# Expert weights in wide row chunks: one group of four chunks for two units of a mixture-of-experts stage

## The chip, the cores and the metric

The kernel runs on one core of a Trainium2 chip. The metric is the device time of one execution in microseconds (us). Before the change the median of three runs is 1634.07 us (1633.24 to 1634.15).

## The reference

Two transformer layers over 512 tokens of width 1024, in float32. Layer 0 is sliding-window attention with a dense SwiGLU; layer 1 is a forgetting attention with a mixture of experts: each token goes to the best 2 of 8 experts. Per expert e and its tokens xb:

```
h = xb @ w_in[e]                      # 1024 -> 2 x 2816 (gate half, up half)
y = (silu(h[:, :2816]) * h[:, 2816:]) @ w_out[e]     # 2816 -> 1024
```

The outputs are weighted with the gates, added per token, and a layer norm closes the layer. The float32 products have to be kept close to float32 accuracy.

## The kernel before, in words

Each float32 matrix is split into a high and a low float16 part, and a product is three matmuls (high·high, high·low, low·high). The weights stream from HBM for this. Class `Weights` (lines 81 to 178) keeps a list of *chunks* of at most 2096 columns per partition. `load` (SP's queue) brings a chunk into a raw buffer (3 buffers, and 4 more in the expert stage); `upper` makes the high part on ScalarE (ACT, line 149), in pieces of 1048 columns; `lower` makes the low part on VectorE (DVE, line 158), one piece behind (`LAG`). The high and low parts live in `NHL` = 7 buffers; a chunk may take a buffer only when the chunk seven places before it has been freed (`W.free`, which sets `done`). `need(i)` demands chunk i before its matmuls.

The conversions have no schedule of their own. The program order is written out by hand: TensorE's (PE's) matmuls are emitted, and between them `tick()` (line 1651) emits one pending small job, one step of `chores`, and one or two conversion pieces: two if fewer than `LEAD` chunks are converted beyond `done`, else one. Each engine then works through its own list in order.

The expert stage (lines 1733 to 1798) runs over 8 expert slots with a fixed number of token columns, `CAP` = 160, 128, 152, 134, 144, 140, 168, 128. A slot's first product is cut in 11 *units*. Units 0 to 9 alternate gate and up, 512 weight columns each: `block4` holds 2 chunks of 4 row blocks x 512 columns, 96 matmuls, 4 ticks. Unit 10 (`gate_pair`) does the last 256 columns of both halves together. After a gate unit ACT applies SiLU to the PSUM result (line 1457); after an up unit DVE multiplies (line 1458), ACT makes the high part and GpSimd (POOL) the low part (line 1460); `pend` holds these and each of the following ticks emits one. The PSUM tile of a unit is reused two units later. Then `down_wide` does the second product, with chunks of 2 row blocks x 1024 columns; the last slot uses `down_direct`.

`chores` (line 1624) is the leftover of the routing: its second step computes the gates (DVE, with one exponential on ACT), its third splits them into three float16 parts (lines 1610 to 1618), the next four scale rows on ACT. `places`, `fetch`, `own_gates` and `ready` prepare the tokens of the next slot after units 2, 4, 6 and 8; `jobs` adds the normalisation of finished rows in the last two slots. When the stage begins, the first three chunks have been loaded and converted by earlier ticks.

Of the kernel before, what the change touches and what calls it, by code (L numbers as in the profile page):

```python
# [8 lines left out]
FT = mybir.dt.float32  # L9
# [11 lines left out]
KD = D // 128  # L21
FF = 2816
# [35 lines left out]
CMAX = max(CAP)  # L58
# [14 lines left out]
BO = "m0mm1m23"  # L73
NHL = 7
LAG = 1
LEAD = 4
QUADS = KF // 4
KG = ((0, 8), (8, 7), (15, 7))


class Weights:
# [87 lines left out]
    def need(self, i):  # L169
        while self.hcut <= i:  # L170
            self.tick(1, force=True)
        while self.cut <= i:
            self.lower()
        return self.chunks[i][3]

    def free(self, u, n=None):

# [32 lines left out]
def trunk_kernel(ctx, tc, x, mem, positions, w_in_swa, attn_sinks, w_in_fox, b_forget, w_mem_kv, w_out,  # L210
                 ln_attn_g, ln_attn_b, w_ffn_in, w_ffn_out, w_router, b_router, w_exp_in, w_exp_out,
                 ln_ffn_g, ln_ffn_b, out):
    nc = tc.nc
# [13 lines left out]
    def bank2():  # L227
        return ps.tile([128, 2, 512], FT, name="bk2", tag="S", bufs=2)

    def high(o, i, scale=1.0):  # L230
        nc.scalar.activation(o, i, AF.Copy, scale=scale)  # L231
# [13 lines left out]
    W = Weights(nc, rawp, hlp)  # L245
# [18 lines left out]
    def unit(u, n):  # L264
        return [View(W, u, i, n) for i in range(2)]
# [33 lines left out]
    u_ei, u_eo = [], []  # L299
    W.from_ = len(W.chunks)  # L300
    def add_exp(s, which, *parts):
        return W.add(*((lambda s=s, k=k, c=c: exp_of(s, which)[:, k[0]:k[1], c[0]:c[1]],
                        (k[1] - k[0]) * (c[1] - c[0])) for k, c in parts))

    for s in range(NEXP):
        u_ei.append([add_exp(s, 0, *[((k, k + 4), (c, c + 512)) for k in (0, 4)])
                     for q in range(QUADS) for c in (512 * q, FF + 512 * q)])
        u_ei[s].append(add_exp(s, 0, *[((0, KD), (c + 512 * QUADS, c + 512 * QUADS + 256)) for c in (0, FF)]))
        if s < LAST:
            u_eo.append([add_exp(s, 1, *[((k, k + 2), (0, D)) for k in range(k0, min(k0 + 4, KF), 2)])  # L310
                         for k0 in range(0, KF, 4)])
        else:
            u_eo.append([add_exp(s, 1, ((k0, k1), (c, c + 512)), ((k1, k0 + kn), (c, c + 512)))
                         for c in (0, 512) for k0, kn in KG for k1 in (k0 + (kn + 1) // 2,)])
# [636 lines left out]
    for i, u in enumerate(u_fi):  # L951
# [16 lines left out]
        else:  # L968
            for jj in range(2):
                f = slice(jj * 128, jj * 128 + 128)  # L970
                b = bank2()
# [417 lines left out]
    def gate_pair(pool, C, w, xe, act, i, tick, nj=2):  # L1389

        wh, wl = w
        b = bank2()
        for jj in range(nj):
            f = slice(jj * 128, jj * 128 + 128)
            for s in range(2):
                for k in range(KD):
                    mm3(b[:, jj, s * C:s * C + C], wh[:, s, k, f], wl[:, s, k, f], xe[0][:, k, :C], xe[1][:, k, :C],
                        k == 0, k == KD - 1)
                tick()

        b = b[:, :nj]
        sa = pool.tile([128, 4, CMAX], FT, name="sa", bufs=nj)[:, :nj]
        j = slice(nj * i, nj * i + nj)

        def first():
            nc.scalar.activation(sa[:, :, :C], b[:, :, :C], AF.Silu, scale=DS)

        def second():
            nc.vector.scalar_tensor_tensor(sa[:, :, :C], b[:, :, C:2 * C], DS * SA, sa[:, :, :C], op0=OP.mult,
                                           op1=OP.mult)  # L1410

        def third():
            high(act[0][:, j, :C], sa[:, :, :C])

        def fourth():
            low(act[1][:, j, :C], sa[:, :, :C], 1.0, act[0][:, j, :C])
        return first, second, third, fourth
# [12 lines left out]
                nc.tensor.matmul(o, wl[:, k, f], act[0][:, kk, :C], start=False, stop=lastk, skip_group_check=True)  # L1430
            tick()

    def block4(C, u, xe, b, tick):

        wh, wl = unit(u, 512)
        for kk in (0, 4):
            for f in range(4):
                o = b[:, f // 2, (f % 2) * C:(f % 2) * C + C]
                c = slice(f * 128, f * 128 + 128)
                for k in range(kk, kk + 4):  # L1440
                    first = k == 0 and f % 2 == 0
                    nc.tensor.matmul(o, wh[:, k, c], xe[0][:, k, :C], start=first, stop=False, skip_group_check=True)  # L1442
                    nc.tensor.matmul(o, wh[:, k, c], xe[1][:, k, :C], start=False, stop=False, skip_group_check=True)  # L1443
                    nc.tensor.matmul(o, wl[:, k, c], xe[0][:, k, :C], start=False, stop=k == KD - 1,  # L1444
                                     skip_group_check=True)
                if f % 2:
                    tick()
            if kk == 0:
                W.free(u, 1)

    def quad(C, b, up, sa, act, q):

        v = b[:, :, :2 * C].rearrange("p a (f c) -> p a f c", c=C)
        sv = sa[:, :, :C].rearrange("p (a f) c -> p a f c", f=2)
        j = slice(4 * q, 4 * q + 4)
        if not up:
            return [lambda: nc.scalar.activation(sv, v, AF.Silu, scale=DS)]
        return [lambda: nc.vector.scalar_tensor_tensor(sv, v, DS * SA, sv, op0=OP.mult, op1=OP.mult),  # L1458
                lambda: high(act[0][:, j, :C], sa[:, :, :C]),
                lambda: nc.gpsimd.tensor_sub(act[1][:, j, :C], sa[:, :, :C], act[0][:, j, :C])]  # L1460

    def down_wide(C, u, act, acc, k0, kn, tick):
        wh, wl = unit(u, D)
# [187 lines left out]
    def tick():  # L1651
        if pend:
            pend.pop(0)()
        next(chores, None)
        W.tick(1 if W.hcut >= W.done + LEAD else 2)

# [76 lines left out]
    for s in range(NEXP):  # L1733
        C = CAP[s]
        act = [mx.tile([128, KF, CMAX], FH, name=f"act{i}", bufs=1) for i in range(2)]
        for i, u in enumerate(u_ei[s]):
            if i < 2 * QUADS:
                if i % 2 == 0:
                    sa = mx.tile([128, 4, CMAX], FT, name="sa", bufs=2)
                b = bank2()  # L1740
                block4(C, u, XE[s], b, tick)
                rest = quad(C, b, i % 2, sa, act, i // 2)
            else:
                rest = gate_pair(mx, C, unit(u, 256), XE[s], act, 2 * QUADS, tick)
            W.free(u)
            pend.extend(rest)
            if (s, i) == (0, 2):
                for _ in range(2):
                    next(chores, None)
                G[0] = own_gates(0, oh, bank())  # L1750
            if (s, i) == (0, 0):
                oh = places(me, lambda t: posm[:, t, 0:1], CAP[0])
            if (s, i) == (0, 1):
                _, _, *at_[0] = fetch(me, oh, blocks(0), False)
            if s + 1 < NEXP:
                if i == 2:
                    oh = places(me, lambda t: posS[:, t, s + 1:s + 2], CAP[s + 1])
                if i == 4:
                    rows, _, *at_[s + 1] = fetch(me, oh, blocks(s + 1))
                if i == 6:  # L1760
                    G[s + 1] = own_gates(s + 1, oh, bank())
                if i == 8:
                    ready(s + 1, rows)
            for f in jobs.get((s, i), ()):
                f()
        if s < LAST:
            acc = [bank() for _ in range(4)]
            for gi, u in enumerate(u_eo[s]):
                kn = min(4, KF - 4 * gi)
                down_wide(C, u, act, acc, 4 * gi, kn, tick)  # L1770
                W.free(u)
                for f in jobs.get((s, 11 + gi), ()):
                    f()
            pend.extend(rows_out(s, C, acc, G[s], at_[s][1]))
        else:
            for gi, u in enumerate(u_eo[s]):
                h, (k0, kn) = gi // 3, KG[gi % 3]
                if k0 == 0:
                    acc = [bank() for _ in range(1 + h)]
                last = k0 + kn == KF  # L1780

                def rest(c0, c1, acc=acc, h=h):
                    for q in range(c0, c1, 256):
                        c, i = slice(512 * h + q, 512 * h + q + 256), 2 * h + q // 256
                        v = acc[1][:, :256] if h and q else acc[0][:, q:q + 256]
                        pend.append(lambda c=c, i=i, v=v: (join(X[s][0], C, c, v, g7[:C, :], st7[:C, 6 * i:6 * i + 6]),
                                                           nc.scalar.activation(yl[:C, c], v[:C], AF.Identity, scale=g7[:C])))
                    if h:
                        late_work()

                down_direct(C, unit(u, 512), act, acc, k0, kn, tick, ((0, 256), (256, 512)) if h else ((0, 512),),
                            rest if last else None)
                W.free(u)
                for f in jobs.get((s, 11 + gi), ()):
                    f()
# [121 lines left out]
```

## Time and profile before

| | |
|---|---|
| median of three runs | 1634.07 us |
| the profiled execution | 1634.23 us, span 1632.4 us |
| mean granted TensorE clock | 0.993 |
| busy: PE, PE weight load, DVE, ACT, POOL | 1578.6, 1267.8, 1210.9, 950.3, 267.7 us |
| HBM read | 355.08 MB |

Times in the profile are microseconds from the span's start. The expert stage takes from 789 us to the end. A busy matmul engine is not one at its peak, since matmuls overlap; the distance from one start to the next says more. A wait is the idle time just before an instruction, with the one whose end released it.

### The profile page before, as it was taken

What the parts mean: (1) busy time and instruction counts of PE and PEld (TensorE: products, weight loads), DVE (VectorE), ACT (ScalarE), POOL (GpSimd) and SP (SyncE); (2) the same over time, 40 slices, a digit from 0 to 9 for tenths busy, and PEclk for the clock granted to TensorE, in tenths of its full rate; (3) what the DMA queues carried; (4) which work ended last, traced back from release to release, by engine and by line L of the source; (5) the groups of instructions that cost most, each with busy time, mean ns of one, the idle gap of its engine ahead of it and who ended that gap; (6) DMA issues with size and microseconds to landing.
All of it is one profiled execution on the core that took longest, in us unless ns stands there. A gap on an engine that the chain in (4) does not pass through costs nothing. (4 is left out here: it accounts for less than half of the span.)

```text
span 1632.4 us, 42978 instructions
## 1 busy us (share of the span) xinstructions
PE 1578.6 (97%) x18640; PEld 1267.8 (78%) x18640; DVE 1210.9 (74%) x1811; ACT 950.3 (58%) x1447; POOL 267.7 (16%) x264
## 2 busy tenths in 40 slices
PE   7998999999999999999899999999999999999996
PEld 6775654444444747765899999999999999999984
DVE  6798543333634568787898798888979889699997
ACT  6676243333211356663676787767877678666773
POOL 0443100000200000003120330203112030130251
PEclk9999999999999999999999999999999999999998
DMA  7511043332631132201899899999999999999993
GB/s 275 178 53 53 27 129 104 103 104 91 219 114 60 53 129 92 66 27 65 308 363 364 293 394 377 352 370 305 390 357 361 375 320 373 329 297 360 358 369 113
DMA packets 180549, 370.16 MB, mean 227 GB/s; under 512 B 6589, under 2 KB 49597, under 8 KB 180352
## 3 DMA queue, kind: packets, MB, share of 16 engines
q1 hardware_dynamic: 173280, 343.48, 58.6%
q0 software_dynamic: 4768, 15.47, 4.0%
q10 hardware_dynamic: 2304, 8.39, 1.4%
q8 instruction: 148, 2.42, 0.6%
q14 instruction: 49, 0.40, 0.1%
HBM read 355.08 MB, written 12.39 MB: 225 GB/s over the span
## 5 line engine op out<-in xcount | busy, mean ns | idle before, releaser
L158 DVE SCALAR_TENSOR_TENSOR wl<-raw,wh 128x1048 f16<-128x1048 f32 (+3 forms) x658 | 794.7, 1258 | 100.3 <-ACT wh L149 100.1
L149 ACT ACTIVATE wh<-raw 128x1048 f16<-128x1048 f32 (+3 forms) x658 | 641.8, 1036 | 101.7 <-PE bk L239 42.9
L1444 PE MATMUL bk<-xa,wl 128*128 128x160 f16 (+3 forms) x1280 | 260.0, 231 | 0.9 <-DVE wl L158 0.9
L1442 PE MATMUL bk<-xa,wh 128*128 128x160 f16 (+3 forms) x1280 | 260.1, 231 | 0.8 <-ACT xa L231 0.8
L1443 PE MATMUL bk<-xa,wh 128*128 128x160 f16 (+3 forms) x1280 | 260.0, 231 | 0.0
L1443 PEld LDWEIGHTS <-wh 128*128 128x128 f16 x2560 | 250.5, 98 | 3.6 <-issue 2.4
L1444 PEld LDWEIGHTS <-wl 128*128 128x128 f16 x2560 | 250.5, 98 | 1.3 <-DVE wl L158 1.1
L1442 PEld LDWEIGHTS <-wh 128*128 128x128 f16 x2560 | 250.4, 98 | 0.7
L1473 PE MATMUL bk<-act,wl 128*128 128x160 f16 (+6 forms) x1232 | 235.3, 227 | 1.2 <-DVE wl L158 1.2
L1472 PE MATMUL bk<-act,wh 128*128 128x160 f16 (+6 forms) x1232 | 235.3, 227 | 0.0
L1471 PE MATMUL bk<-act,wh 128*128 128x160 f16 (+6 forms) x1232 | 235.2, 227 | 0.0
L1442 PE MATMUL bk<-xe,wh 128*128 128x128 f16 (+2 forms) x1280 | 223.2, 221 | 2.2 <-DVE sa L1458 1.4
L1443 PE MATMUL bk<-xe,wh 128*128 128x128 f16 (+2 forms) x1280 | 223.1, 221 | 0.0
L1444 PE MATMUL bk<-xe,wl 128*128 128x128 f16 (+2 forms) x1280 | 223.1, 221 | 0.0
L237 PE MATMUL bk<-xTh,wh 128*128 128x512 f16 (+2 forms) x656 | 204.8, 322 | 1.2 <-DVE Kx L234 0.9
L239 PE MATMUL bk<-xTh,wl 128*128 128x512 f16 (+2 forms) x656 | 204.6, 322 | 1.4 <-DVE wl L158 1.4
L238 PE MATMUL bk<-xTl,wh 128*128 128x512 f16 (+2 forms) x656 | 204.6, 322 | 0.5 <-DVE xTl L234 0.5
L1460 POOL TENSOR_TENSOR act<-sa,act 128x512 f16<-128x512 f32 (+6 forms) x40 | 106.3, 2659 | 284.7 <-ACT act L231 284.6
L239 PEld LDWEIGHTS <-wl 128*128 128x128 f16 x944 | 92.4, 98 | 49.0 <-DVE wl L158 2.9
L237 PEld LDWEIGHTS <-wh 128*128 128x128 f16 x944 | 92.4, 98 | 48.7 <-ACT wh L149 2.0
L238 PEld LDWEIGHTS <-wh 128*128 128x128 f16 x944 | 92.5, 98 | 46.6 <-issue 1.5
L1473 PEld LDWEIGHTS <-wl 128*128 128x128 f16 x1232 | 120.5, 98 | 1.6 <-DVE wl L158 1.6
(349 smaller groups left out, 2669.2 us busy)
## 6 DMA issues: line engine op xcount, KB each, us to landing
raw<-in_w_exp_in_dram SPq DMA_DIRECT2D x176, 1024.0 KB
raw<-in_w_exp_out_dram SPq DMA_DIRECT2D x85, 1024.0 KB
raw<-in_w_ffn_in_dram SPq DMA_DIRECT2D x22, 1024.0 KB
raw<-in_w_out_dram SPq DMA_DIRECT2D x8, 1024.0 KB
raw<-in_w_ffn_out_dram SPq DMA_DIRECT2D x8, 1024.0 KB
raw<-in_w_in_fox_dram SPq DMA_DIRECT2D x8, 1024.0 KB
raw<-in_w_in_swa_dram SPq DMA_DIRECT2D x4, 896.0 KB
raw<-in_w_mem_kv_dram SPq DMA_DIRECT2D x3, 1024.0 KB
```

The lines of the kernel that those rows point to most:

```text
L149: self.nc.scalar.activation(h[:, p:e], t[:, p:e], AF.Copy, scale=SW)
L158: self.nc.vector.scalar_tensor_tensor(l, src, SW, h, op0=OP.mult, op1=OP.subtract)
L237: nc.tensor.matmul(o, lh, rh, start=first, stop=False, **kw)
L238: nc.tensor.matmul(o, lh, rl, start=False, stop=False, **kw)
L239: nc.tensor.matmul(o, ll, rh, start=False, stop=last, **kw)
L1442: nc.tensor.matmul(o, wh[:, k, c], xe[0][:, k, :C], start=first, stop=False, skip_group_check=True)
L1443: nc.tensor.matmul(o, wh[:, k, c], xe[1][:, k, :C], start=False, stop=False, skip_group_check=True)
L1444: nc.tensor.matmul(o, wl[:, k, c], xe[0][:, k, :C], start=False, stop=k == KD - 1, skip_group_check=True)
L1460: lambda: nc.gpsimd.tensor_sub(act[1][:, j, :C], sa[:, :, :C], act[0][:, j, :C])]
L1471: nc.tensor.matmul(o, wh[:, k, c], act[0][:, kk, :C], start=first, stop=False, skip_group_check=True)
L1472: nc.tensor.matmul(o, wh[:, k, c], act[1][:, kk, :C], start=False, stop=False, skip_group_check=True)
L1473: nc.tensor.matmul(o, wl[:, k, c], act[0][:, kk, :C], start=False, stop=kk == KF - 1, skip_group_check=True)
```

## The change

The first product of a slot is no longer cut in 11 units of 2 chunks. Its columns fall into three groups (1024, 1024, 768 wide), each with a gate half and an up half. One half of a group is one unit of four chunks, each 2 row blocks x the group's width. It serves two blocks: the first 512 columns, and then the rest (512, or 256 in the last group). The chunks are freed one by one during the second block. A slot so has 12 blocks in the order gate, gate, up, up for each group; the last two columns of row blocks, 256 columns, are a block of their own in the gate and in the up half, and go through `quad`, so that POOL and no longer DVE makes their low part. `LEAD` rises from 4 to 6. A block of 256 columns has 2 ticks in place of 4. `need_high` and `passes` are added, but no call uses them with other than the default.

```diff
-LEAD = 4
+LEAD = 6
+GROUPS = ((0, 1024), (1024, 1024), (2048, 768))
...
-        u_ei.append([add_exp(s, 0, *[((k, k + 4), (c, c + 512)) for k in (0, 4)])
-                     for q in range(QUADS) for c in (512 * q, FF + 512 * q)])
-        u_ei[s].append(add_exp(s, 0, *[((0, KD), (c + 512 * QUADS, c + 512 * QUADS + 256)) for c in (0, FF)]))
+        u_ei.append([add_exp(s, 0, *[((k, k + 2), (c, c + n)) for k in range(0, KD, 2)])
+                     for c0, n in GROUPS for c in (c0, FF + c0)])
...
+    def blocks_of(C, u, n, c0, nb, xe, b, tick, passes=(0, 1, 2)):
+        for kk in range(0, KD, 2):
+            a = W.first[u] + kk // 2
+            wh = W.need_high(a) if 2 not in passes else W.need(a)[0]
+            wl = None if 2 not in passes else W.need(a)[1]
+            for f in range(nb):
+                o = b[:, f // 2, (f % 2) * C:(f % 2) * C + C]
+                for k in (kk, kk + 1):
+                    c = (k - kk) * n + c0 + f * 128
+                    for p in passes:
+                        w = (wl if p == 2 else wh)[:, c:c + 128]
+                        nc.tensor.matmul(o, w, xe[p == 1][:, k, :C], start=p == 0 and k == 0 and f % 2 == 0,
+                                         stop=p == 2 and k == KD - 1, skip_group_check=True)
+            if nb == 4 or kk % 4:
+                tick()
+            if c0 + nb * 128 == n and 2 in passes:
+                W.free(u, kk // 2 + 1)
...
-                block4(C, u, XE[s], b, tick)
-                rest = quad(C, b, i % 2, sa, act, i // 2)
-            else:
-                rest = gate_pair(mx, C, unit(u, 256), XE[s], act, 2 * QUADS, tick)
-            W.free(u)
-            pend.extend(rest)
+        halves_of = [(u_ei[s][2 * g + up], n, c, min(4, (n - c) // 128), up, (c0 + c) // 128)
+                     for g, (c0, n) in enumerate(GROUPS) for up in range(2) for c in range(0, n, 512)]
+        sas = {}
+        for i, (u, n, c, nb, up, j0) in enumerate(halves_of):
+            if not up:
+                sas[j0] = mx.tile([128, 4, CMAX], FT, name="sa", bufs=2)
+            b = bank2()
+            blocks_of(C, u, n, c, nb, XE[s], b, tick)
+            pend.extend(quad(C, b, up, sas[j0], act, j0, nb))
...
-            for f in jobs.get((s, i), ()):
+            for f in jobs.get((s, i), ()) if i < 11 else ():
```

## Rows read from the trace of the kernel before

**Rows 1.** Windows, one: busy us (instructions) of PE, PEld, DVE, ACT, POOL; clock, DMA, GB/s
```profile
1100.00:1200.00 100.00, 100.00 (x1690) 99.56 (x1688) 86.32 (x90) 77.20 (x95) 20.56 (x9) 1.00 0.99 355
```
**Rows 2.** PE's waits, 786 to 1430 us, the longest: total, times, longest
```profile
PE bk L1444 <- DVE wl L158: 0.9, 1, 0.9
```
**Rows 3.** PE's waits, 1430 us to the end, all of them
```profile
PE bk L1518 <- DVE wl L158: 4.4, 3, 3.9
PE bk L1442 <- DVE sa L1458: 1.4, 1, 1.4
PE bk L1473 <- DVE wl L158: 1.2, 2, 0.9
PE bk L1442 <- ACT sa L1457: 0.8, 1, 0.8
```
**Rows 4.** Timeline of PE, first two units of the stage: start, duration, [idle before]
```profile
789.18 0.23 PE L1443 MATMUL bk<-xa,wh 128*128 128x160 f16 x1
...
799.56 0.23 PE L1443 MATMUL bk<-xa,wh 128*128 128x160 f16 x1
800.66 0.24 PE L1444 MATMUL bk<-xa,wl 128*128 128x160 f16 x1 [0.87 <-DVE wl L158]
...
804.30 1.00 PE L1351 MATMUL bk<-tid,oh 128*128 128x2 f16 x8 [0.70 <-DVE oh L1339]
805.23 0.24 PE L1442 MATMUL bk<-xa,wh 128*128 128x160 f16 x1
```
**Rows 5.** Waits of SP's DMA queue, 820 us to the end, the longest
```profile
SPq L122 <- DVE wl L158: 586.5, 233, 8.6
```
**Rows 6.** Timeline of DVE, first two units of the stage
```profile
796.11 1.25 DVE L158 SCALAR_TENSOR_TENSOR wl<-raw,wh 128x1048 f16<-128x1048 f32 x1
797.28 0.42 DVE L1162 TENSOR_TENSOR g<-ose,gateE 128x256 f32<-128x256 f32 x1
...
799.41 2.35 DVE L158 SCALAR_TENSOR_TENSOR wl<-raw,wh 128x1000 f16<-128x1000 f32 x2
```
**Rows 7.** Timeline of ACT, first two units of the stage
```profile
795.02 2.96 ACT L149 ACTIVATE wh<-raw 128x1048 f16<-128x1048 f32 x3
```
**Rows 8.** Windows (columns as in rows 1) around PE's two longest gaps
```profile
777.40:779.80 2.40, 0.00 (x0) 0.00 (x0) 2.29 (x8) 0.00 (x0) 0.00 (x0) 1.00 0.93 320
780.30:783.50 3.20, 3.20 (x36) 2.86 (x35) 1.55 (x3) 1.77 (x4) 2.31 (x2) 0.50 1.05 396
...
1606.30:1609.60 3.30, 3.11 (x16) 1.98 (x15) 3.27 (x5) 0.18 (x1) 3.30 (x1) 0.50 0.00 0
```
**Rows 9.** DVE's groups by shape, from 740 us: count, busy us, mean ns, idle before
```profile
L158 DVE SCALAR_TENSOR_TENSOR wl<-raw,wh 128x1048 f16<-128x1048 f32 x262 | 354.8, 1354 | 67.0 <-ACT wh L149 66.9
...
L158 DVE SCALAR_TENSOR_TENSOR wl<-raw,wh 128x488 f16<-128x488 f32 x4 | 2.6, 658 | 0.0
```
**Rows 10.** Timeline of DVE in slot 1 (128 columns)
```profile
917.82 5.85 DVE L158 SCALAR_TENSOR_TENSOR wl<-raw,wh 128x1000 f16<-128x1000 f32 x4
...
924.42 4.62 DVE L158 SCALAR_TENSOR_TENSOR wl<-raw,wh 128x1000 f16<-128x1000 f32 x4
928.96 0.68 DVE L1458 SCALAR_TENSOR_TENSOR sa<-bk,sa 128x512 f32<-128x512 f32 x1
```
**Rows 11.** Timeline of POOL in the same stretch
```profile
919.80 1.64 POOL L1460 TENSOR_TENSOR act<-sa,act 128x512 f16<-128x512 f32 x1
```
**Rows 12.** DVE's groups, 1446.7 to 1616.5 us, the costliest
```profile
L158 DVE SCALAR_TENSOR_TENSOR wl<-raw,wh 128x1000 f16<-128x1000 f32 (+1 forms) x103 | 124.6, 1264 | 5.0 <-ACT wh L149 5.0
```
**Rows 13.** Timelines at block 7 of slot 6: PE's last lookup before it, DVE
```profile
1453.44 0.24 PE L1668 MATMUL bk<-parts,oh 128*128 128x3 f16 x4
...
1454.60 0.15 DVE L1672 TENSOR_REDUCE gown<-bk 128x1 f32<-128x3 f32 x1
```
**Rows 14.** Windows of 5 us in slot 2 (columns as in rows 1)
```profile
1045.00:1050.00 5.00, 5.00 (x80) 5.00 (x78) 3.51 (x5) 2.91 (x4) 0.49 (x1) 1.00 1.01 406
...
1055.00:1060.00 5.00, 5.00 (x77) 4.98 (x78) 4.79 (x8) 5.00 (x9) 0.00 (x0) 1.00 0.68 243
```

More of the change, by code (lines that the diff above doesn't have):

```diff
@@ L174, in need, with need_high @@
         return self.chunks[i][3]
+    def need_high(self, i):
+        while self.hcut <= i:
+            assert self.upper(True)
+        return self.chunks[i][3][0]
     def free(self, u, n=None):
@@ L1431, in down_group, with quad @@
             tick()
[L1433 to L1437, printed above, removed]
-                o = b[:, f // 2, (f % 2) * C:(f % 2) * C + C]
[L1439 to L1455, printed above, removed]
+    def blocks_of(C, u, n, c0, nb, xe, b, tick, passes=(0, 1, 2)):
[4 more added lines that the diff above has]
+            for f in range(nb):
+                o = b[:, f // 2, (f % 2) * C:(f % 2) * C + C]
+                for k in (kk, kk + 1):
[8 more added lines that the diff above has]
+                W.free(u, kk // 2 + 1)
+    def quad(C, b, up, sa, act, j0, nb):
+        v = b[:, :nb // 2, :2 * C].rearrange("p a (f c) -> p a f c", c=C)
+        sv = sa[:, :nb, :C].rearrange("p (a f) c -> p a f c", f=2)
+        j = slice(j0, j0 + nb)
         if not up:
@@ L1458, in quad @@
         return [lambda: nc.vector.scalar_tensor_tensor(sv, v, DS * SA, sv, op0=OP.mult, op1=OP.mult),
-                lambda: high(act[0][:, j, :C], sa[:, :, :C]),
-                lambda: nc.gpsimd.tensor_sub(act[1][:, j, :C], sa[:, :, :C], act[0][:, j, :C])]
+                lambda: high(act[0][:, j, :C], sa[:, :nb, :C]),
+                lambda: nc.gpsimd.tensor_sub(act[1][:, j, :C], sa[:, :nb, :C], act[0][:, j, :C])]
     def down_wide(C, u, act, acc, k0, kn, tick):
@@ L1735, in trunk_kernel @@
         act = [mx.tile([128, KF, CMAX], FH, name=f"act{i}", bufs=1) for i in range(2)]
[L1736 to L1740, printed above, removed]
-                block4(C, u, XE[s], b, tick)
-                rest = quad(C, b, i % 2, sa, act, i // 2)
-            else:
-                rest = gate_pair(mx, C, unit(u, 256), XE[s], act, 2 * QUADS, tick)
-            W.free(u)
-            pend.extend(rest)
+        halves_of = [(u_ei[s][2 * g + up], n, c, min(4, (n - c) // 128), up, (c0 + c) // 128)
[7 more added lines that the diff above has]
+            pend.extend(quad(C, b, up, sas[j0], act, j0, nb))
             if (s, i) == (0, 2):
```

## The prediction, made before the run

> **What bounds the kernel now.** I read the busy table by windows first: in the expert stage PE is busy all the time at full clock, its weight loads too, DVE for 86 of 100 us, ACT for 77, and the DMA engines' share is 0.99 [rows 1]. Three engines and the DMA look full, so the table alone does not name the bound. The list of PE's waits does. Between 786 and 1430 us the longest wait on a conversion is 0.9 us [rows 2], and the whole last part holds 4.4 + 1.4 + 1.2 + 0.8 = 7.8 us [rows 3]. Matmuls of 160 columns start every (799.56 - 789.18) / 150 = 0.0692 us [rows 4], so they stand end to end; for 128 columns I scale to 0.0554 and for 168 to 0.0727. PE's column count is the bound, and the change leaves the number of matmuls and columns as it is. The loads are behind: SP's queue waits 586 us for a raw buffer to be given back [rows 5]. So the change can win only in the few waits, some 9 us in all, and it can lose wherever it starves PE. Three places decide: the start, the slots of 128 columns, and the end, where DVE falls behind.
>
> **The start: a loss.** Three chunks are converted when the stage begins. Before, two chunks fed a block of 96 matmuls, so three lasted one and a half blocks: chunk 3 was first wanted by block 1, and its second piece by matmul 153 (96 + 48 + 9). PE got there at 799.6 and waited to 800.66 [rows 4], since DVE's second piece of chunk 3 runs from 799.41 to about 800.6 [rows 6]. In the new form block 0 goes through all four chunks itself. Chunk 3 is wanted after 72 matmuls, at 789.18 + 71 x 0.0692 = 794.1. The tick that emits its conversion is the same one, after 24 matmuls, with the same chores ahead of it, so it comes no earlier: ACT's first piece is done at 795.02 + 2.96 / 3 = 796.0 [rows 7], DVE's at 797.4, then the third step of the chores takes DVE from 797.28 to 799.4, and the second piece ends at 800.6 [rows 6]. Of the first row block PE can do three matmuls in between, of the second two; the 78th matmul waits for 800.66. That leaves 19 of block 0 and 96 of block 1: 115 x 0.0692 = 7.96, so block 1 ends at 808.6. The token lookup then takes 805.23 - 804.30 = 0.93 [rows 4] and does not wait for DVE any more, as it did for 0.70. Block 2 starts at 809.5 and not at 805.23: **4.3 us lost**. Chunks 4 to 7 are late by nothing: their eight pieces and the four one-hot masks follow on DVE at 1.2 us a piece and end near 812, while chunk 7 is wanted at 814.
>
> There is a second cost. PE stood still for 2.4 us from 777.4, and then ran at a granted clock of 0.50 (1.2 GHz, not 2.4) for 3.2 us; after the 3.9 us gap at 1602 it ran at 0.50 for 3.3 us [rows 3, 8]. The new gap, 794.1 to 800.66 with five matmuls in it, is longer than both. If the half clock falls on the stretch after the gap, 3.4 us of it cost 1.7; if it falls into the gap, nothing. I take **1.7**, as both rows have it after the gap. The start costs 6.0 (4.3 to 6.0).
>
> **The other edits, stage in full run.** The elements converted are the same. A slot gets 8 chunks of 1536 columns (pieces of 1048 and 488) for 6 of 2048, so 4 pieces more. A piece of 488 columns takes 0.658 us and one of 1048, undisturbed, 1.25 [rows 6, 9]: (1.25 - 0.658) / 560 = 0.00106 per column, so 0.14 of the 0.658 are the piece's own, some 0.6 us per slot on DVE (1.354, the mean of all pieces of 1048, would make 0.05 of it) and nothing on PE as long as DVE keeps ahead. The low part of the last 256 columns moves from DVE (about 0.45 us, estimated from the multiplication 0.68 us at 512) to POOL. That is no plain gain: four DVE pieces take 4.62 us when alone, 5.85 when POOL's subtraction of 1.64 us lies in them [rows 10, 11], so a full subtraction holds DVE for 1.2 and one of half the size for about 0.6.
>
> In a slot of 128 columns a block takes 96 x 0.0554 = 5.3 us. The seven buffers now come free only in second halves, at 1.3, 2.7, 4.0 and 5.3 us of it. DVE begins with the first freed buffer after ACT's piece (1.3 + 0.1 + 1.1 = 2.5), does four pieces, 1.2 each, up to 7.4, and a subtraction may add 1.2; then comes the multiplication (0.7) of the block just ended, at 8.1 to 9.3. PE wants its PSUM tile back two blocks on, at 10.7. The margin is 1.4 to 2.6 us, and DVE is already behind by one or two us there: the multiplication at 928.96 starts without any wait for PE [rows 10]. I take **1.0** for all slots together; bounds are 0 (the margin holds) and 1.5 us for each of two groups in slots 1, 3, 4 and 5, 12 us.
>
> In the second product the larger `LEAD` puts 5 to 6 converted chunks ahead of PE, by a count of the ticks in the code, where it had 3 to 4. PE has two waits for low parts there, 1.2 us [rows 3]; they are in the sum of the end.
>
> **The end.** From slot 6 on DVE is the late engine: of 170 us from 1446.7 on it waits 5.0 for high parts [rows 12], and all PE's waits but one are for DVE [rows 3]. Here DVE's sum counts. When PE starts block 7 of slot 6 the new order has 19 chunks of the slot converted, the old 17 and a half: 1.5 x 2.4 = 3.6 us by a count of the ticks, and 1 us more since the old DVE is only then done with block 6's pieces (1454.6, PE's block begins at 1453.5 [rows 13]). Taken off: one more multiplication with its subtraction still to do (0.85 + 1.2), 8 pieces' overhead (1.2), two half subtractions (1.2) less the two low parts (0.9), and a new idle of 2.0, as the first buffer is freed 24 x 0.0727 = 1.7 us into the block and ACT needs 1.1, DVE having 0.85 of other work. Gains 5.5, costs 6.5. That is even within what such a sum is good for: **0**, bounds -9.5 (all 7.8 of waits and the 1.7 of half clock go) and +3.
>
> **Sum.** 1634.2 (the profiled execution, its span of 1632.4 and 1.8 around it, 0.2 above the median) + 6.0 + 1.0 + 0 = 1641.2 us.
>
> **A page on the loads.** The chunk's rows grow from 2 to 4 KB. At full demand the loads moved 406 GB/s in 5 us, and 243 where buffers were short [rows 14]. The Trainium skill, "DMA: Bandwidth & Descriptors", section "Where 436 GB/s comes from", puts HBM's limit per core at about 358 GB/s. By that rule the stage's 355 GB/s would be the bound, and rival 4 would hold; the trace does not agree, as it shows 406 over 5 us.
>
> **Rivals.**
> 1. *The deeper lead clears the end.* Against it: DVE's sum, not the order, sets that end. For it: two waits for low parts with DVE work between the pieces [rows 3]. Price: 7.8 + 1.7 back, 1641.2 - 9.5 = 1631.7, and 1630.0 if the half clock at the start is not paid. It ends faster than before once more than 7 us come back. Chance 0.15.
> 2. *The bunched conversions starve PE in the narrow slots.* 12 us in place of 1: 1652; half of it 1647. For it, DVE already late in slot 1; against it, PE has not one wait there now. Chance 0.13.
> 3. *The start does not stall*, because chunk 3 is converted sooner than I read, or the change does not act there as I think. Then 1634.2 + 1.0 - 0.9 - 0.7 = 1633.6. Chance 0.12.
> 4. *The loads set the pace*, and a gap of PE at the start is made up while they run on: 1634. The row with 243 GB/s under a busy PE speaks against it [rows 14]. Chance 0.05.
>
> The forecast has 0.55, with a range of its own from 1637.5 to 1645.
>
> **Chances.** About 0.2% (3.3 us) is what a measurement tells from no change: below 1630.8 faster, above 1637.3 slower. Faster: a third of rival 1, some of 3, and 0.04 for what I do not see, 0.12. Slower: the forecast's bulk and rival 2, 0.60. Same: the rest, 0.28. The range of 8 in 10 runs from 1632 to 1648.
>
> **What would show it.** Right: PE idle between 794 and 801 in block 0 of the first slot, waiting for `wl`; half clock behind it; block 2 near 809.5. PE's waits on the multiplication only in narrow slots, after an up block. At the end PE's waits add up to about the same. Wrong: no gap at the start; a last slot without waits for DVE; new waits of PE in every slot, above all at first blocks of a group.

## The result, and the profile after

The kernel after takes 1642.69 us (median of four runs, 1641.88 to 1643.38), beside 1633.65 for the kernel before in the same comparison (1633.15 to 1634.15). The ratio is 1.0052, 95% interval 1.004 to 1.0065: slower by 9 us. The profiled execution took 1641.88 us, its span 1639.8; mean granted clock 0.990.

To see where the time went I took, from the timelines of PE in both traces, the first matmul of each slot's first and second product, and formed the distance after minus before. A change of the distance from one mark to the next is what that stretch costs. Worked out in this way, in us, good to about 0.1:

| stretch | predicted | measured |
|---|---|---|
| ahead of the stage | 0 | -0.9 |
| slot 0, first product (the start) | +6.0 | +5.4 |
| slot 1, first product (128 columns) | +1.0 in all narrow slots | +0.7 |
| slots 2 to 5, first product of slot 6 | 0 | 0.0 |
| slot 6, second product | in the end's sum | -1.6 |
| slot 7, first product | in the end's sum | +5.9 |
| slot 7, second product, to the last instruction | in the end's sum | -2.1 |
| the end together | 0 | +2.2 |

The -0.9 lies ahead of the stage, where neither the new blocks nor `LEAD` act. Over the traces of this study the stage began between 785.6 and 788.9 us, the 788.9 being the kernel before's [rows 4]; I count from the stage's own start, which gives +8.3.

PE's waits, first from 780 to 1433 us and then from there to the end (total, times, longest), answer to [rows 2] and [rows 3]:

```profile
PE bk L1451 <- DVE wl L160: 3.6, 2, 2.7
PE bk L1451 <- ACT wh L151: 1.9, 1, 1.9
PE bk L1451 <- ACT xa L238: 0.8, 1, 0.8
PE bk L1451 <- DVE sa L1465: 0.7, 1, 0.7
...
PE bk L1499 <- ACT yt L1492: 2.9, 1, 2.9
PE bk L1525 <- DVE wl L160: 2.1, 2, 1.7
PE bk L1451 <- DVE wl L160: 1.5, 2, 0.8
PE bk L1451 <- DVE sa L1465: 0.3, 1, 0.3
```

The first two rows are the start, `xa` is the wait ahead of the stage's first matmul, the `sa` of 0.7 is slot 1, and `yt` is new: it is the lift of slot 6's output rows, in which ACT copies them out of PSUM for PE's transposes. The start in PE's timeline, beside [rows 4]:

```profile
795.23 0.31 PE L1451 MATMUL bk<-xa,wh 128*128 128x160 f16 x2 [1.88 <-ACT wh L151]
...
796.51 0.31 PE L1451 MATMUL bk<-xa,wl 128*128 128x160 f16 x1 [0.97 <-DVE wl L160]
...
799.75 0.31 PE L1451 MATMUL bk<-xa,wl 128*128 128x160 f16 x1 [2.66 <-DVE wl L160]
...
809.37 0.42 PE L1357 MATMUL bk<-tid,oh 128*128 128x2 f16 x8
809.72 0.31 PE L1451 MATMUL bk<-xa,wh 128*128 128x160 f16 x2
```

DVE's timeline, beside [rows 6], shows what it did while PE waited: the first piece of chunk 3, the chores' third step, and only then the second piece.

```profile
795.20 1.25 DVE L160 SCALAR_TENSOR_TENSOR wl<-raw,wh 128x1048 f16<-128x1048 f32 x1
796.37 0.42 DVE L1168 TENSOR_TENSOR g<-ose,gateE 128x256 f32<-128x256 f32 x1
...
798.41 0.20 DVE L1623 CAST parts<-gateS 128x32 f16<-128x32 f32 x1
798.50 5.74 DVE L160 SCALAR_TENSOR_TENSOR wl<-raw,wh 128x1000 f16<-128x1000 f32 x5
```

Windows of the start, beside [rows 8] (PE, PEld, DVE, ACT, POOL, then granted clock, DMA share, GB/s): the clock falls to 0.50 at 796.4, while PE still stands in the second of its three waits, and stays there until 803.2, some 3.4 us behind the last wait.

```profile
796.40:799.80 3.40, 0.63 (x4) 0.32 (x5) 3.16 (x11) 3.40 (x4) 0.00 (x0) 0.50 0.04 17
799.80:803.20 3.40, 3.40 (x27) 3.40 (x28) 3.40 (x4) 3.38 (x5) 0.00 (x0) 0.50 0.69 200
```

The new wait at slot 7's begin, in ACT's timeline. The store of normalised rows stands in ACT's list and waits for DVE's norm; behind it stand ten high pieces, and behind them the lift:

```profile
1524.61 0.34 ACTq L1715 DMA_DIRECT2D out_dram<-xtok  x1
1525.05 9.58 ACT L151 ACTIVATE wh<-raw 128x1048 f16<-128x1048 f32 x10 [4.10 <-PE bk L1480]
1534.54 0.76 ACT L1492 ACTIVATE yt<-bk 128x336 f32<-128x336 f32 x2
```

PE needs `yt` at 1535.02, after 2.94 us of waiting, and then has half the clock (window 1535 to 1540; in the one before it the clock fell, 0.87 in the mean):

```profile
1535.00:1540.00 5.00, 4.98 (x39) 4.81 (x40) 4.97 (x6) 3.86 (x7) 0.00 (x0) 0.50 1.03 416
```

### The profile page after: what moved, and what is told of

It reads as the page before. It is cut to its first block, busy times and chain, and to the rows that moved or that the text cites. A ratio compares the mean times of both kernels' runs of the same rounds, so it can differ in the third digit from the quotient of the medians.

```text
span 1639.8 us, 43254 instructions
## 1 busy us (share of the span) xinstructions
PE 1583.0 (97%) x18640; PEld 1271.9 (78%) x18640; DVE 1203.9 (73%) x1835; ACT 954.9 (58%) x1479; POOL 215.6 (13%) x272
## 3 DMA queue, kind: packets, MB, share of 16 engines
q8 instruction: 148, 2.42, 0.6%
## 5 line engine op out<-in xcount | busy, mean ns | idle before, releaser
L160 DVE SCALAR_TENSOR_TENSOR wl<-raw,wh 128x1048 f16<-128x1048 f32 (+4 forms) x690 | 788.8, 1199 | 119.4 <-ACT wh L151 119.0
L151 ACT ACTIVATE wh<-raw 128x1048 f16<-128x1048 f32 (+4 forms) x690 | 645.1, 995 | 128.3 <-PE bk L246 42.7
L1451 PEld LDWEIGHTS <-wh 128*128 128x128 f16 x5632 | 454.2, 98 | 5.1 <-ACT wh L151 2.1
L1451 PE MATMUL bk<-xa,wh 128*128 128x160 f16 (+3 forms) x2816 | 290.1, 232 | 2.7 <-ACT wh L151 1.9
L1451 PE MATMUL bk<-xa,wl 128*128 128x160 f16 (+3 forms) x1408 | 287.2, 232 | 3.6 <-DVE wl L160 3.6
L1451 PE MATMUL bk<-xe,wh 128*128 128x128 f16 (+2 forms) x2816 | 249.1, 222 | 1.0 <-DVE sa L1465 1.0
L1451 PE MATMUL bk<-xe,wl 128*128 128x128 f16 (+2 forms) x1408 | 246.9, 222 | 1.6 <-DVE wl L160 1.5
L1478 PEld LDWEIGHTS <-wh 128*128 128x128 f16 x1232 | 120.6, 98 | 0.0
L1479 PEld LDWEIGHTS <-wh 128*128 128x128 f16 x1232 | 120.5, 98 | 0.0
L1467 POOL TENSOR_TENSOR act<-sa,act 128x512 f16<-128x512 f32 (+13 forms) x48 | 65.4, 1363 | 393.7 <-ACT act L238 393.7
L244 PEld LDWEIGHTS <-wh 128*128 128x128 f16 x688 | 67.3, 98 | 48.2 <-ACT wh L151 1.4
L245 PEld LDWEIGHTS <-wh 128*128 128x128 f16 x688 | 67.4, 98 | 46.6 <-issue 1.5
L952 DVE SCALAR_TENSOR_TENSOR av<-bk,sa 128x512 f32<-128x512 f32 x22 | 15.2, 692 | 114.8 <-ACT sa L951 114.8
```

The lines of the kernel that those rows point to most:

```text
L151: self.nc.scalar.activation(h[:, p:e], t[:, p:e], AF.Copy, scale=SW)
L160: self.nc.vector.scalar_tensor_tensor(l, src, SW, h, op0=OP.mult, op1=OP.subtract)
L244: nc.tensor.matmul(o, lh, rh, start=first, stop=False, **kw)
L245: nc.tensor.matmul(o, lh, rl, start=False, stop=False, **kw)
L952: nc.vector.scalar_tensor_tensor(av, b[:, 1, :], DS * SA, sa, op0=OP.mult, op1=OP.mult)
L1451: nc.tensor.matmul(o, w, xe[p == 1][:, k, :C], start=p == 0 and k == 0 and f % 2 == 0, stop=p == 2 and k == KD - 1, skip_group_check=True)
```

## The experiments

All were timed beside the kernel before, whose median in these comparisons was 1633.25 to 1633.71 us. What each stretch of PE cost against the profiled execution of before, formed as above, in us:

| kernel | start | slot 1 | slot 6, 2nd | slot 7, 1st | slot 7, 2nd, to the end | median |
|---|---|---|---|---|---|---|
| after | +5.4 | +0.7 | -1.6 | +5.9 | -2.1 | 1642.69 |
| e1 chores later | +1.8 | +0.7 | -1.6 | +5.9 | -2.1 | 1637.33 |
| e2 LEAD 4 | +5.9 | 0.0 | +1.5 | +0.6 | -0.3 | 1641.45 |
| e3 before, LEAD 6 | +3.9 | 0.0 | -1.6 | +5.8 | -6.0 | 1634.13 |
| e4 stores on POOL | +5.4 | +0.7 | -1.6 | +2.8 | +0.9 | 1641.78 |
| e5 stores on SP | +6.3 | +0.8 | -1.6 | +2.8 | -2.8 | 1638.94 |
| e6 before, chores later | -1.5 | 0.0 | +0.3 | 0.0 | +0.7 | 1632.55 |
| e7 before, LEAD 6, both edits | +5.9 | 0.0 | -1.6 | -0.5 | -6.4 | 1630.22 |
| e9 old shape in slots 6, 7 | +5.5 | +0.8 | -1.6 | +5.2 | -5.9 | 1637.50 |
| e8 new chunks, all edits | +0.8 | +0.8 | -1.6 | +2.8 | -2.8 | 1632.97 |
| e10 old chunks, all edits | -1.5 | +0.8 | -1.6 | -0.9 | -6.0 | 1623.93 |
| e11 e10 with LEAD 4 | -1.5 | 0.0 | -1.6 | -0.9 | +0.3 | 1629.80 |
| e12 e10 with late return | -1.5 | +0.8 | -1.6 | -1.8 | -4.5 | 1624.05 |

After, e2, e4, e5 and e9 have nearly the same three waits at the start (5.5 to 5.7 us together) and yet cost 5.4 to 6.3: what differs is how much of the half clock falls behind the last wait. In e5 it is 5.4 us, in after 3.4:

```profile
799.90:805.30 5.40, 5.40 (x41) 5.40 (x42) 5.40 (x9) 5.37 (x7) 0.00 (x0) 0.50 0.82 283
```

So differences under 1 us between two starts say nothing about an edit.

**e1, the start.** Nothing of the chores is emitted during block 0.

```diff
-        next(chores, None)
+        if not hold:                # cleared after block 0 of slot 0
+            next(chores, None)
```


> The kernel after, with the routing chores (gates, their three parts, four row scalings) not stepped during block 0 of slot 0; they begin with block 1. Theory: the start's loss of 5.4 us (PE's starts of slot 0's second product: +4.5 against before, after +(-0.9) at the stage's start) comes from those 4 to 5 us of DVE work that stand ahead of chunk 3's low part. Then PE has no gap between 794 and 800, no half clock behind it, and the time falls by 3.5 to 5.4 us, to 1637.3 to 1639.2; a smaller gap at chunk 7 (about 807) may remain. Rival: the three chunks converted ahead are the cause by themselves, ACT and DVE cannot bring chunk 3 by 794 whatever stands ahead: the gap stays over 3 us and the time within 1.5 us of 1642.7.

Measured: 1637.33 us, 5.4 less than after. In the traces the start costs 1.8 in place of 5.4, 3.6 less; the two profiled runs, 1641.88 and 1638.34, are also nearer to each other than the medians. No wait of 2 us is left:

```profile
PE bk L1451 <- DVE sa L1465: 2.0, 3, 0.8
PE bk L1451 <- DVE wl L160: 2.0, 2, 1.5
```

The chores ahead of chunk 3 are the cause of the stop there. The rest, waits of 1.5 and 0.4 at 807 to 810, is chunk 7, as expected; that the multiplication is late too (two of the waits on `sa`, at 819 and 827; the third is slot 1's) was not.

**e2 and e3, the lead and the shape apart.**

```diff
-LEAD = 6
+LEAD = 4     # e2: in the kernel after.  e3: 4 -> 6 in the kernel before
```


> The kernel after with LEAD back at 4. Theory A (the larger lead puts more conversions ahead of the row norms, and ACT's in-order stores then hold its lift of the rows): slot 7's first product gets back its 5.9 us (no wait of PE for yt at its start, no half clock there), slot 6's second product loses its gain of 1.6 again and the last one its 2.1: about 1640.5 (1637.5 to 1642.5). The start's 5.4 stays. Rival (the chunks' shape, with DVE's extra pieces, is the cause): PE still waits for yt, the time stays at 1642.7 within 1 us, or is longer by new waits for low parts at the starts of groups.

> The kernel before with LEAD = 6 alone. Theory A: the lead by itself brings the wait for yt at the start of slot 7 and a half clock behind it: 1635 to 1639, and the start of the stage unchanged. Rival (shape is the cause): no wait for yt, 1633.65 within 1 us, or some us less if the deeper lead takes away the waits for low parts at the end.

Measured: e2 1641.45, e3 1634.13. PE's waits from 1433 us on, e2:

```profile
PE bk L1525 <- DVE wl L160: 4.2, 2, 3.9
PE bk L1451 <- DVE wl L160: 2.3, 4, 0.8
PE bk L1480 <- DVE wl L160: 2.1, 2, 1.2
```

and e3:

```profile
PE bk L1492 <- ACT yt L1485: 4.2, 1, 4.2
PE bk L1442 <- ACT sa L1457: 0.8, 1, 0.8
PE bk L1518 <- DVE wl L158: 0.3, 1, 0.3
```

The wait for the lift belongs to the lead: it comes with LEAD = 6 in the old shape and goes with LEAD = 4 in the new one. Theory A holds on the place. Its sizes were off: in e2 the waits come back as waits for low parts and the end stays at +1.8, and in e3 the last product gives 6.0 back, so that the whole is not told from no change (ratio 1.0005, 0.9996 to 1.0014). e3 also has a wait of 3.0 us for the one-hot masks at its start, which I had not expected. Slot 1's 0.7 us is in neither.

**e4 and e5, the stores away from ACT.**

```diff
-        nc.scalar.dma_start(out[0, t * 128:(t + 1) * 128, :], xtok[:, t, :])
+        nc.gpsimd.dma_start(...)    # e4;  e5: nc.sync.dma_start(...)
```


> The kernel after with the four stores of normalised rows (slot 6) issued on POOL's queue and not on ACT's. Theory: ACT held by the store until 1524.6 is what makes the high pieces and the lift late. With the stores elsewhere ACT is free from about 1505 on, PE's wait of 2.9 us for yt and the half clock behind it go, slot 7's first product gets back 4 to 6 us: 1637 to 1639. Rival: DVE's sum sets that stretch (pieces and norms end to end); ACT comes earlier, but PE then waits for wl by as much: 1641.5 to 1643.

> The kernel after with the four stores of normalised rows on SP's queue. With the stores on POOL's queue PE's last matmul came 2.9 us earlier (1624.8 against 1627.7), but the program ended as late, 8.7 us behind the last POOL instruction instead of 5.8. Theory A: ACT's hold is worth about 3 us, and those stores on POOL's queue lengthened the end by as much; on SP's queue the end is 5.8 us again: about 1639.8 (1638.8 to 1640.8). Rival: something else than POOL's queue ends the program late, the 3 us are lost again: 1641.8 within 0.8. SP's order is DVE's own order, so no load should be held by a store.

Measured: e4 1641.78, e5 1638.94. In both the wait for `yt` is gone and slot 7's first product costs 2.8 in place of 5.9. In e4 POOL's last instruction starts 2.9 us sooner than in after (1633.29 there), but the span ends at 1639.9:

```profile
1630.41 0.76 POOL out_dram L1698
```

The span ends 8.7 us behind that instruction; with the stores on SP it is 5.7, in the kernel after 5.8. So ACT's hold is worth 3 us and more, and e4's median alone would have told the opposite. What lengthens the end when POOL's queue issues the stores, the traces don't show. In e5 SP's queue stands 13.2 us in all at the four stores, waiting for DVE's norms, and ACT once 3.1 us for a load, so the expectation that SP's queue would not be held did not come true; the gain is what is left after that.

**e6, the chores in the kernel before.** The edit of e1.

> The kernel before with the routing chores held until unit 0 of slot 0 is emitted. Theory: the old start has only 0.9 + 0.7 us of waits to lose, so 0.5 to 1.6 us less, 1632.2 to 1633.2 by the last comparison's 1633.25 for before; the chores cost the new shape 5.4 us because there chunk 3 is wanted 5.5 us sooner. Rival: the chores by themselves cost any order some 5 us: 1628.

Measured: 1632.55; ratio 0.9993, interval 0.9984 to 1.0002, so not told from no change by itself, while the trace has the start 1.5 us shorter. The old order had little to lose there.

**e7, old chunks with LEAD = 6 and both edits.**

> The kernel before (old chunks) with LEAD = 6, the stores on SP's queue, and the chores held during unit 0. With LEAD = 6 alone the stages stood against before: start +3.9 (a wait of 3.0 us for the one-hot masks), second product of slot 6 -1.6, first product of slot 7 +5.8 (a wait of 4.2 us for the lift, half clock behind it), last product -6.0. Theory: the chores' hold takes away the start's loss (to +1 at most), ACT free of the stores takes 3 to 5 us from slot 7's first product, and the last product keeps most of its gain: 1627 to 1630. Rival: the end is DVE's sum, what slot 7's first product gets back the last product loses in waits for low parts: 1630.5 to 1632.

Measured: 1630.22, just above the theory's range; ratio 0.9976 (0.9967 to 0.9985). The end goes as the theory says: the rival's giving back doesn't come. The start doesn't: it costs 5.9. In DVE's list the third step of the chores now ends at 808.3, four low pieces follow to 812.8, and only then comes unit 1's multiplication, for which PE waits; the half clock follows. DVE's row, and PE's:

```profile
813.25 0.81 DVE L1458 SCALAR_TENSOR_TENSOR sa<-bk,sa 128x640 f32<-128x640 f32 x1
```
```profile
814.11 0.31 PE L1442 MATMUL bk<-xa,wh 128*128 128x160 f16 x1 [5.33 <-DVE sa L1458]
```

**e9, the old shape in slots 6 and 7 of the kernel after.**

```diff
-        u_ei.append([... new groups ...])
+        if s < 6: u_ei.append([... new groups ...])
+        else:     u_ei.append([... 2 chunks of 4 x 512 ...])   # block4, gate_pair
```


> The kernel after, with the old chunks and units (2 chunks of 4 row blocks x 512, freed one by one in each unit) in slots 6 and 7 alone; LEAD stays at 6. Theory: from slot 6's second product to the end the new shape costs 4.0 us at LEAD = 6 (PE's offset against before goes from 5.2 to 7.4 in the kernel after and from 2.6 to 0.8 in the old shape with LEAD = 6), since buffers freed only in second halves leave DVE idle (6.6 us of 36 from 1451, 1.7 before). With the old shape there: about 1638.7 (1637.7 to 1639.7), a wait for the lift at slot 7's start of 3 to 4 us as with the old shape at LEAD = 6. Rival: the tail's loss comes from the lead and from what went before: 1642 to 1643.

Measured: 1637.50, 5.2 less than after and just below the theory's range; the wait for the lift is there (3.6 us), and the last product is at -5.9 as in e3. The shape costs some 4 to 5 us at the end.

**e10, e8 and e11: all edits with old and new chunks.** Chores held in block 0, stores on SP's queue, and the lead by slot:

```diff
+        lead[0] = 6 if s else 4     # e11: 4 throughout
```


> Old chunks; chores held during unit 0, stores of normalised rows on SP's queue, lead 4 in slot 0 and 6 from slot 1 on. Theory: the three effects add up, since they lie in different stretches: start -1.5 as with the chores held alone at lead 4, the end's -8.4 as seen with lead 6 and the stores on SP's queue (slot 6's second product -1.6, slot 7's first -0.5, last -6.4): about 1624 (1623 to 1626). Rival: the end's gain at lead 6 hung on the 5.9 us that PE lost at the start there (a later PE lets the conversions run ahead): then the end gives back that much, 1628.5 to 1630.

> New chunks with the same three edits: chores held during block 0, stores on SP's queue, lead 4 in slot 0 and 6 from slot 1 on. Theory: the gains measured one by one, 5.4 for the chores and 3.8 for the stores, add up: 1633.5 (1632 to 1635), and what lies between this and the old chunks with the same edits, some 9 us, is the price of the shape itself: buffers given back in second halves only, and chunk 3 wanted in block 0. Rival: with the conversions' order mended the shape costs nothing of its own: within 2 us of the old chunks with the same edits.

> Old chunks, chores held during unit 0, stores on SP's queue, LEAD = 4 throughout. Theory: at lead 4 ACT's hold by the stores delays nothing that PE waits for (no wait for the lift in the kernel before; its waits at the end are for low parts, DVE's sum), so about as with the chores held alone, 1632.5 (1631 to 1633.5). Rival: the stores' hold delays the high pieces, and with them DVE, at lead 4 too: 1626 to 1629.

Measured: e10 1623.93, ratio to before 0.9941 (0.9928 to 0.9955), which beats both kernels; e8 1632.97, ratio 0.9996 (0.9986 to 1.0005); e11 1629.80, ratio 0.9977 (0.9967 to 0.9987). All waits of PE in the expert stage of e10, beside the nine us of [rows 2, 3]:

```profile
PE bk L1442 <- ACT sa L1457: 1.4, 2, 0.8
PE bk L1442 <- DVE sa L1458: 1.4, 2, 0.9
PE bk L1442 <- ACT xa L231: 0.8, 1, 0.8
PE bk L1518 <- DVE wl L158: 0.4, 1, 0.4
```

The effects add up as the theory for e10 and e8 said, and with all other edits equal the new chunks cost 1632.97 - 1623.93 = 9.0 us: by the traces 2.3 at the start, 3.7 in slot 7's first product, 3.2 behind it. For e11 my theory was wrong: the stores' hold cost the kernel before 2.7 us at LEAD = 4 too (1632.55 to 1629.80). Its wait of 3.9 for low parts stays, and that one the lead takes away. In e10 the old chunks lose 0.8 us in slot 1 too, there in a wait for ACT's SiLU and not for the multiplication, though not in e3 and e7.

The 6.9 us behind slot 6 show in the waits: from slot 7's start on PE waits 5.8 us for DVE in e8 and 0.8 in e10, where ACT adds 0.8, so 4.2 more; and in e8 the clock is at 0.50 from 1540.8 to 1544.3, just behind the second of these waits, which costs some 1.7. The last 1.0 us of the 6.9 these figures do not show.

**e12, what of the new shape costs at the end.** e10, with two units' buffers given back only in the second unit, in slots 6 and 7.

```diff
                 if f % 2:
                     tick()
+                    if late:
+                        W.free(u - 1, kk // 2 + f // 2 + 1)
-            if kk == 0:
+            if kk == 0 and late is None:
                 W.free(u, 1)
```


> The fastest kernel so far (old chunks, chores held, stores on SP's queue, lead 6 from slot 1; 1623.9 us), with one thing of the new shape put in, in slots 6 and 7 alone: two units' four buffers are given back only in the second unit, one after each of its four ticks, as the new blocks do. Chunks, pieces and the multiplications stay as they are. With these edits the new shape lost against the old 3.7 us in slot 7's first product and 3.2 us in the last product. Theory: the buffers' late return is the cause; DVE idles in the first blocks and is late by that at the end: 1627.5 to 1631. Rival: the eight more pieces, the changed order of chunks, and POOL's two more subtractions are the cause, and the return is free: 1623.5 to 1625.

Measured: 1624.05, as e10 (ratio to before 0.9942, 0.9928 to 0.9956). So the buffers' late return by itself, with the old chunks, costs nothing that the medians tell. But the edit did not bring about the idling of DVE that it was made for. Over slot 6's first product DVE stands for 12.6 us in e10, 15.1 in e12 and 18.3 in e8; in the last 36 us of it for 2.2, 1.7 and 6.6. Windows of these 36 us (the third number is DVE's), e10, e12, e8:

```profile
1444.80:1480.80 36.00, 36.00 (x498) 35.99 (x497) 33.79 (x41) 24.69 (x28) 8.78 (x8) 1.00 1.04 325
```
```profile
1445.13:1481.13 36.00, 36.00 (x499) 35.99 (x497) 34.26 (x41) 24.41 (x28) 9.23 (x8) 1.00 1.04 331
```
```profile
1446.60:1482.60 36.00, 36.00 (x498) 35.99 (x496) 29.37 (x43) 24.56 (x31) 7.76 (x7) 1.00 1.04 324
```

What e12 adds lies in the first part of the slot. In e8's 6.6 us DVE waits 3.4 for ACT's high parts and once 2.9 for PE's lookup of the gates; in e12 these are 0.7 and nothing. So the theory falls for the return alone, and what idling of this kind costs with the new chunks is not tested. What the new chunks leave undone shows in DVE's low pieces from PE's begin of slot 7 to the end, by shape (count, busy us, mean ns). e10:

```profile
L158 DVE SCALAR_TENSOR_TENSOR wl<-raw,wh 128x1048 f16<-128x1048 f32 x30 | 39.1, 1303 | 2.6 <-ACT wh L149 2.6
L158 DVE SCALAR_TENSOR_TENSOR wl<-raw,wh 128x1000 f16<-128x1000 f32 x26 | 30.9, 1187 | 0.0
L158 DVE SCALAR_TENSOR_TENSOR wl<-raw,wh 128x488 f16<-128x488 f32 x4 | 3.0, 743 | 0.0
```

and e8:

```profile
L160 DVE SCALAR_TENSOR_TENSOR wl<-raw,wh 128x1048 f16<-128x1048 f32 x34 | 42.3, 1245 | 3.3 <-ACT wh L151 3.3
L160 DVE SCALAR_TENSOR_TENSOR wl<-raw,wh 128x1000 f16<-128x1000 f32 x23 | 28.3, 1230 | 0.0
L160 DVE SCALAR_TENSOR_TENSOR wl<-raw,wh 128x488 f16<-128x488 f32 x12 | 10.1, 843 | 0.0
```

Columns still to convert: 30 x 1048 + 26 x 1000 + 4 x 488 = 59,392 against 64,488, so 5,096 more in e8, and nine pieces more; DVE's time for them is 73.0 against 80.7. These 7.7 us stand beside the 6.9 us that e8 loses from there on; that they are the cause is likely, but argued from the two sizes. (In e12 it is 60,392 columns.) So the new chunks bring PE to slot 7 with 3,096 columns ahead of it (67,584, both products of slot 7, less 64,488) and the old ones with 8,192; when slot 6's second product began it was 5,144 against 8,192 already. Which property leaves them behind was not separated: buffers that hold 1,536 columns in the last group and not 2,048, the order of chunks in a group, the extra block, or the late return together with one of these. Only the late return with the old chunks is excluded.

## Why the prediction came out as it did

**The bound** was right: slots 2 to 5, where PE's matmuls stand end to end [rows 1, 4], cost nothing, and all of the loss lies at the start, in slot 1 and in the end, in PE's waits and the half clock behind them. Rival 4 is out: the gap at the start was not made up behind it.

**The start** was right in mechanism and size, 5.4 against 6.0, and e1 shows the cause. PE stopped at the first piece of chunk 3 and at its second piece, resumed at 799.75 (predicted 800.66, with a stage begin 0.9 later), and the 115 matmuls from there to the lookup took 9.62 us and not 7.96: 1.66 for the half clock, predicted 1.7. What was off is the lookup, 0.35 us and not 0.93, which is the 0.6 between the two sums. I had read the 0.93 in [rows 4] as matmuls, but four of them came one by one as DVE made the four one-hot masks:

```profile
803.95 0.93 DVE L1339 TENSOR_SCALAR oh<-iota_c,posm 128x160 f16<-128x160 f32 x4
```

That the half clock came out at 1.7 was partly luck: it lasted 6.8 us and half of that fell into the waits; in e5 more of it fell behind them. Rival 3 is out.

**The narrow slots** took 0.7, predicted 1.0, but only in slot 1, for the multiplication as named. The shape alone doesn't bring it: with LEAD = 4 it is 0.0 (e2). The prediction did not tie it to the lead. Rival 2 is out.

**The end** was taken as even and cost 2.2, inside its bounds of -9.5 to +3; the sum came out near by luck, two errors against each other (+5.9 against -1.6 and -2.1). The step on the second product, which put the larger lead at 5 to 6 chunks and counted only 1.2 us of waits, failed: those are chunks in program order. By the low pieces that DVE had done, PE began slot 6's second product with 5,144 columns ahead (2.5 chunks; before: 4,096, 2.0), and slot 7 with 2,048 (before 3,096). And it left out who stands behind the added pieces: ACT's stores wait for norms that now come behind more pieces, and the lift waits behind the stores. After, the fourth store leaves ACT 1.1 us before PE begins slot 7 (1525.74); before, it left 7.7 us ahead (1522.12):

```profile
1514.38 0.34 ACTq L1708 DMA_DIRECT2D out_dram<-xtok  x1
```

Of the 5.9 us the wait for the lift is 2.9 and the half clock behind it at least 2.5 (0.50 over the five us of the window above); e5 took off 3.1 in all. The idle that I put at 2.0 us for DVE was 6.6 - 1.7 = 4.9 more than before, in the last 36 us of slot 6's first product; what it cost by itself no run shows.

Rival 1, that the deeper lead clears the end, was right on the lead and wrong for this kernel. With old chunks it takes 6 us from the last product (e3), and with the stores out of ACT's list 8.5 from the whole end (e10), of the 9.5 that the rival named; here the hold of ACT and the shape gave it back.

**POOL and the pieces.** I charged half subtractions with holding DVE, and extra pieces with their overhead. DVE's sum did not change. [rows 9] and the shape between them there, all from 740 us on, add up to 354.8 + 312.9 + 2.6 = 670.3 us before; after it is 348.7 + 266.7 + 54.6 = 670.0, with 32 pieces more. The row between, before, and the three after:

```profile
L158 DVE SCALAR_TENSOR_TENSOR wl<-raw,wh 128x1000 f16<-128x1000 f32 x258 | 312.9, 1213 | 9.4 <-ACT wh L149 9.4
```
```profile
L160 DVE SCALAR_TENSOR_TENSOR wl<-raw,wh 128x1048 f16<-128x1048 f32 x278 | 348.7, 1254 | 87.7 <-ACT wh L151 87.5
L160 DVE SCALAR_TENSOR_TENSOR wl<-raw,wh 128x1000 f16<-128x1000 f32 x210 | 266.7, 1270 | 7.8 <-ACT wh L151 7.8
L160 DVE SCALAR_TENSOR_TENSOR wl<-raw,wh 128x488 f16<-128x488 f32 x68 | 54.6, 803 | 0.3 <-ACT wh L151 0.2
```

The pieces of 1048 are shorter in the mean than before, those of 1000 and 488 longer. Taken by themselves, the pieces beside which POOL does nothing last the same in both kernels: 1.24, 1.19 and 0.66 us in the mean. So what POOL's work adds has only moved from the pieces of 1048 to the other two. By these means the 32 pieces cost DVE some 5 us, 0.16 each where I had 0.14, and POOL's work adds some 5 us less.

## What to carry to other kernels

A lead in program order is no lead in time: count what the converting engine has really finished when the consumer gets there, and look at what else each in-order engine has behind the work moved forward. A store issued from a compute engine waits in that engine's list for its data; moved to a queue whose order already agrees with the data's, it gave 2.7 us or more here, though SP's queue then waited at the stores. Where a loss moves from wait to wait under single edits, only the sum over the stretch counts: on the old kernel the lead alone lost 0.9 us and the chores alone gained 1.1, neither told from no change, the stores on top of the chores gained 2.7, and all three together, with the lead raised only from slot 1 on, 9.8.

## What the runs showed of the hardware

The same subtraction of 128x512 on POOL took 3.86 us in the mean of ten before and 1.30 after (times on POOL are rough). The kernel before, and after:

```profile
L1460 POOL TENSOR_TENSOR act<-sa,act 128x512 f16<-128x512 f32 x10 | 38.6, 3864 | 39.6 <-ACT act L231 39.6
```
```profile
L1467 POOL TENSOR_TENSOR act<-sa,act 128x512 f16<-128x512 f32 x10 | 13.0, 1302 | 70.7 <-ACT act L238 70.7
```

Before, the ten range from 1.15 us, where DVE did nothing, to 9.36, where it went from piece to piece without a gap. DVE pays too: of the four pieces in the 5.85 us of [rows 10], the one that meets the subtraction of [rows 11] took 2.42 us, the other three 1.19 to 1.24:

```profile
920.08 2.42 DVE L158 SCALAR_TENSOR_TENSOR wl<-raw,wh 128x1000 f16<-128x1000 f32 x1
```

In the new order DVE's idle time ahead of its pieces of 1048 rose from 67.0 to 87.7 us [rows 9], and a subtraction can fall into it. So the first one of slot 1 does after, for the most part, where [rows 10, 11] had it inside DVE's pieces. POOL's row, and DVE's:

```profile
930.80 1.16 POOL L1467 TENSOR_TENSOR act<-sa,act 128x512 f16<-128x512 f32 x1 [6.66 <-ACT act L238]
```
```profile
931.64 4.79 DVE L160 SCALAR_TENSOR_TENSOR wl<-raw,wh 128x1048 f16<-128x1048 f32 x4 [1.66 <-ACT wh L151]
```

The Trainium skill, "SBUF — State Buffer", section "SBUF: two separate sides", says that the two engines share a port pair as an exclusive lock, also for a VectorE operation with two SBUF inputs against a GpSimd operation that reads SBUF, and that whoever starts first keeps it for the whole instruction. The rows agree with that: a subtraction that begins while DVE stands takes 1.16 us, and one that meets DVE's work makes one piece 1.2 us longer or is itself drawn out.

In the stage of the kernel after, PE's granted clock was at 0.50 (1.2 GHz) three times before PE's last matmul. At the start it fell at 796.4, in the second of three waits of 1.88, 0.97 and 2.66 us with two and three matmuls between them, and rose at 803.2. At slot 7's start it fell inside the wait of 2.94 us and was still 0.50 over the window from 1535 to 1540. The third time, from 1619.0 to 1622.4, followed a wait of 1.74 us. The sum of the start needed that term: 1.66 us.
